# A hybrid GLA and mLSTM block: value blocks in tags of their own, values in four pieces, weight loads behind value transfers

## The chip, the cores and the metric

The kernel runs on one core of one Trainium2 chip. The metric is the device time of the core in microseconds (us). Engines: PE multiplies matrices, DVE, ACT and POOL work on vectors, SP issues most DMA transfers. Each engine works through its own instructions in the order of the program, and waits for another only through semaphores.

## The reference

One layer of a decoder trunk on 1024 tokens and 16 learned meta tokens in front (1040 rows of width 1024). Token mixing has two branches of four heads each, GLA and mLSTM, both in chunks of tokens that carry a matrix state on; then gates, a merge, and a feed-forward part with a causal convolution.

```python
# GLA, one chunk
inter = jnp.einsum('bhtk,bhkv->bhtv', qc * jnp.exp(bc), S)
scores = jnp.einsum('bhtk,bhsk,bhtsk->bhts', qc, kc, decay)
out = inter + jnp.einsum('bhts,bhsv->bhtv', scores, vc)
S_new = exp(b_last) * S + jnp.einsum('bhsk,bhsv->bhkv', kc * jnp.exp(b_last - bc), vc)
# mLSTM, one chunk
num = w_inter * jnp.einsum('bhtk,bhkv->bhtv', qc, C_prev) + jnp.einsum('bhts,bhsv->bhtv', qk, vc)
C_new = g_prev * C_prev + jnp.einsum('bhs,bhsk,bhsv->bhkv', w_state, kc, vc)
```

Both take values `v` of 256 columns per head, with tokens on the rows.

## The kernel before

Projections are computed with three matmuls per block of 128: the high part of the input by the high part of the weight (xH, wH), then xL by wH and xH by wL, in one accumulation. A weight block arrives as `wr` (512 KB, one DMA on SP, two buffers), ACT casts it to `wH` (L152), DVE subtracts to get `wL` (L153). That is `prep` (L141 to L153).

The stage of the heads takes the first 590 us. Its eight heads (0 to 3 GLA, 4 to 7 mLSTM) follow one another: `value_proj(s)` (it runs `proj_v`, L263), then `key_query_proj(s + 1)`. These are generators that PE works on at full density. At every `yield` the function `main` (L1226) adds a number to an account, `due`, and for every whole unit takes one step of other work (`advance`, L1214): one step of `closing` (`post`: scaling, turning and storing a finished head) and one of `side` (`gla` or `mlstm` of a head whose keys, queries and values are there). PACE is 1.15. A half piece of values counts `share` = 9/4 n/T, where n is the columns of the piece and T is 1040; its six pieces and halves yield twice each, which makes 10.35 steps for the values of a head, and the six yields of keys and queries make 6.9.

Values come out of `proj_v` with channels on the rows and have to be turned. Per head there are three pieces of the token axis, VSEG, of 400, 384 and 256 columns, and two halves of 128 channels (`j`). A half piece is 24 matmuls into `pv` (L281), an eviction by ACT into `vs` (L285), a turn of 32 x 32 blocks by DVE into `vr` (L287 and L288), stores of `vr` to DRAM on SP (L298, L301), and a load back into `v` (L306) with tokens on the rows. The `vr` blocks have the tag "r" with two buffers; the turned outputs `of` of `post` (L782) have the same tag, so a new `vr` waits for the stores of an `of` (L792), and the other way round.

In a GLA head the scores of a chunk are made by levels 1, 2, 4, ..., 64. A level is: two subtractions on DVE (L952, L953), an exponent on ACT (L954), a product in two halves on POOL and DVE (L956) and one on DVE (L957) that give `pk`; then four matmuls into `sc` on PE (L904), and a masked copy into A on DVE (L923). `sct` (L893) turns A when all levels up to 16 are in. After the last chunk `post` takes rstd of the head by POOL's power (L124), scales eight blocks on ACT (L773) and the row `om` (L774).

In an mLSTM head keys and queries go through a convolution of three operations on DVE (L1105), the rows MB and WB of the gates are broadcast from DRAM by SP (L1097, L1099), and then eight chunks follow: a state update matmul `up` (L1156), two output matmuls `op` (L1188, L1189), DVE's update of the state C (L1186) and copy of `dn` (L1191), ACT's copy and square (L1190, L1192). Two chunks are one step.

A scheduler sets the order of each engine from the order of the program, priorities (`hp`) and its own estimate of when things are ready; `behind_all` and `issue_after` keep an instruction behind another. The order is fixed when the program is built.

Of the kernel before, what the change touches and what calls it, by code (L numbers as in the profile page):

```python
# [9 lines left out]
F32 = mybir.dt.float32  # L10
# [7 lines left out]
P = 128  # L18
D = 1024
NM = 16  # L20
SEQ = 1024
T = NM + SEQ
NK = D // P
# [4 lines left out]
DV = 256  # L28
# [12 lines left out]
SEG_ALL = [(0, 272), (272, 256), (528, 256), (784, 256)]  # L41
# [4 lines left out]
def hybrid_kernel(ctx, tc, x, meta, norm_mix, w_in, b_in, gla_w_gate, gla_b_gate, gla_norm,  # L46
                  ml_conv_w, ml_conv_b, ml_norm, w_branch_gla, w_branch_ml, w_out, norm_ffn,
                  ffn_w_up, ffn_conv_w, ffn_conv_b, ffn_w_down, norm_final, out):
    nc = tc.nc
    x, out = x[0], out[0]  # L50
    w_in, b_in = w_in[0], b_in[0]
# [7 lines left out]
    def hp(n):  # L59

        return tc.high_priority(offset=max(1, min(n, tc.cur_priority - floor[0])))
# [56 lines left out]

    def rstd_of(ss, n, w, pool, name):

        v = pool.tile([P, w], F32, name=name + "v", tag="rv", bufs=4)
        nc.vector.tensor_scalar(v, ss, 1.0 / n, EPS, OP.mult, OP.add)
        r = pool.tile([P, w], F32, name=name + "r", tag="rr", bufs=4)
        rooted[:] = [nc.gpsimd.tensor_tensor(r, v, mhalf.to_broadcast([P, w]), OP.pow)]  # L124
        return r

# [6 lines left out]
    def behind_all(ins):  # L133
        es = ExitStack()
        for i in ins:
            es.enter_context(tc.issue_after(i))
        return es

    parted = []

    def prep(src, shape, name):  # L141

        if name == "gk1":
            raw = hd.tile([P, T], F32, name="wr_" + name, tag="raw", bufs=1)[:, :NK * P].rearrange(
                "p (k n) -> p k n", n=P)
        else:
            raw = wp.tile(shape, F32, name="wr_" + name, tag="wr", bufs=2)
        nc.sync.dma_start(raw, src)
        wH = wp.tile(shape, F32R, name="wH_" + name, tag="wH")
        wL = wp.tile(shape, F32R, name="wL_" + name, tag="wL")  # L150
        with behind_all(held):
            nc.scalar.activation(wH, raw, AF.Copy)  # L152
            parted[:] = [nc.vector.tensor_tensor(wL, raw, wH.bitcast(F32), OP.subtract).ins]  # L153
        return wH, wL
# [53 lines left out]
    def wsrc(w, k0, nk, n0, n):  # L208
        return w[k0 * P:(k0 + nk) * P, n0:n0 + n].rearrange("(k p) n -> p k n", p=P)
# [45 lines left out]
                    continue  # L255
                yield

    VSEG = [(0, 400), (400, 384), (784, 256)]
    hsc = dram.tile([NC, P, D], F32, name="hsc")
    vsc = [hsc[2 * (s % H):2 * (s % H) + 2].rearrange("a p (x w) -> (a p x) w", w=DV).rearrange("(b i) w -> b i w", i=32)  # L260
           for s in range(2 * H)]
# [1 line left out]
    def proj_v(s, us, vt):  # L263

        U.get(us[0])
        U.get(us[1], 1)
        due_load = []
        for g, (t0, n) in enumerate(VSEG):
            nb, b0 = n // 32, max(t0 - NM, 0) // 32
            at, share = 1 if g == 0 else 0, 9 / 4 * n / T  # L270
            R = hd.tile([P, T], F32, name=f"vr{s}_{g}", tag="r", bufs=2)[:, :64 * (nb + at)].rearrange(
                "p (b t j) -> p b t j", t=2, j=32)
            for j in range(2):
                wH, wL = U.got[us[j]]
                pt = ps.tile([P, 512], F32, name=f"pv{us[j]}_{g}", tag="pj", bufs=3)
                i = 0
                for k in range(NK):
                    if k == NK // 2:
                        yield share
                    for a, b in ((wH, xH), (wH, xL), (wL, xH)):  # L280
                        nc.tensor.matmul(pt[:, :n], a[:, k, :], b[:, k, t0:t0 + n], start=(i == 0), stop=(i == 3 * NK - 1))  # L281
                        i += 1
                with hp(PRI_E):
                    S = hd.tile([P, 400], F32, name=f"vs{us[j]}_{g}", tag="vs", bufs=2)
                    kept_ = nc.scalar.activation(S[:, :n], pt[:, :n], AF.Identity, bias=vbias[:, 2 * s + j:2 * s + j + 1])  # L285
                    if at:
                        nc.vector.transpose(R[:, 0, j, :], S[:, :32])  # L287
                    turned_ = nc.vector.transpose(R[:, at:, j, :], S[:, NM * at:n].rearrange("p (b j) -> p b j", j=32))  # L288
                    hold(turned_.ins, kept_.ins)
                    evicts.append(kept_.ins)  # L290
                if j == 0:
                    for load in due_load:
                        load()
                    due_load.clear()
                yield share
            for q in range(4):
                cols = slice(64 * q, 64 * q + 64)
                nc.sync.dma_start(vsc[s][b0:b0 + nb, :, cols].rearrange("b i w -> i b w"),  # L298
                                  R[32 * q:32 * q + 32, at:].rearrange("p b t j -> p b (t j)"))
                if at:  # L300
                    nc.sync.dma_start(vt[:NM, 0, cols], R[32 * q:32 * q + NM, 0].rearrange("p t j -> p (t j)"))  # L301

            def load(g=g, t0=t0, n=n):
                c = 0 if g == 0 else (t0 - NM) // P
                m = n // P
                nc.sync.dma_start(vt[:, 1 + c:1 + c + m, :DV],  # L306
                                  vsc[s][4 * c:4 * (c + m)].rearrange("(c b) i w -> (b i) c w", b=4))
            due_load.append(load)
        late_loads.extend(due_load)

# [39 lines left out]
    def rows(dst, ap, off, n):  # L350
        small.append((dst, bass.AP(tensor=ap.tensor, offset=ap.offset + off, ap=[[P, n], [1, P]])))

    va = hd.tile([P, DV + 1], F32, name="va", tag="S", bufs=4)[:, :P]
    segs = [(b_in, O_GQ, 8), (b_in, O_GR, 8), (b_in, O_MQ, 8), (b_in, O_MO, 8), (b_in, O_GA, 16), (gla_norm, 0, 2),
            (ml_conv_w, 0, 32), (ml_conv_b, 0, 8), (ml_norm, 0, 8)]
    at, nrow = [], 0
# [441 lines left out]
    A0 = hd.tile([P, P], F32, name="A0", tag="wg", bufs=1)  # L798

    def state(name):  # L800
        return hd.tile([P, DV + 1], F32, name=name, tag="S", bufs=4)

    def first_decay():

# [44 lines left out]
    def gla(s):  # L849
# [189 lines left out]
        up = upd(0)  # L1039
        om = hd.tile([2, DV + 1], F32, name=f"om{s}", tag="om", bufs=1)  # L1040
        ss = hd.tile([P, NC + 1], F32, name=f"ss{s}", tag="ss", bufs=2)
        junk = hd.tile([P, DV], F32, name=f"junk{s}", tag="junk", bufs=1)
        nc.vector.memset(ss, 1.0)
        yield
        op = ps.tile([P, 2, DV], F32, name=f"omp{s}", tag="ot", bufs=2)
# [39 lines left out]
    def mlstm(s):  # L1085
# [77 lines left out]
        om = hd.tile([2, W1], F32, name=f"om{s}", tag="om", bufs=1)  # L1163
        ss = hd.tile([P, NC + 1], F32, name=f"ss{s}", tag="ss", bufs=2)
        dn = hd.tile([P, NC + 1], F32, name=f"dn{s}", tag="dn", bufs=2)
        junk = hd.tile([P, DV], F32, name=f"junk{s}", tag="junk", bufs=1)
        nc.vector.memset(ss, 1.0)
        nc.vector.memset(dn, 1.0)
        up = upd(0)
# [54 lines left out]
    due = [0.0]  # L1224

    def main(gen, pace=PACE):  # L1226
        for share in gen:
            for load in late_loads:
                load()
            late_loads.clear()  # L1230
            due[0] += pace * (share or 1)
            while due[0] >= 1:
                due[0] -= 1
                advance()
# [3 lines left out]
    for s in range(8):  # L1238
        if s:
            side.append((gla if s < 4 else mlstm)(s))  # L1240
        if s == 3:
            side.append(small_rows())
        main(value_proj(s))
        if s < 7:
            main(key_query_proj(s + 1))
    for j in TAIL:
        main(merge_gate_b(j))
    while side or closing:
# [62 lines left out]
    def gate_weights(q):  # L1311

        rg, ru = (gs.tile([P, NK, P], F32, name=f"gw{i}{q}", tag="wr3") if (2 * q + i) % 3 == 2 else
                  wp.tile([P, NK, P], F32, name=f"gw{i}{q}", tag="wr", bufs=2) for i in range(2))
        for r, g in ((rg, GATES[2 * q]), (ru, GATES[2 * q + 1])):
            nc.sync.dma_start(r, wsrc(w_in, 0, NK, g[0], P))
        def split(src, h, l):
            nc.scalar.activation(h, src, AF.Copy)
            nc.vector.tensor_tensor(l, src, h.bitcast(F32), OP.subtract)

        def place(name):
            nonlocal ngw
            ngw += 1
            if ngw % 4 == 3:
                return [gs.tile([P, NK, P], F32R, name=f"g{p}{name}_{q}", tag="w4" + p) for p in "HL"]
            return [wp.tile([P, NK, P], F32R, name=f"g{p}{name}_{q}", tag="w" + p) for p in "HL"]

        def halves(t):
            return [(t[0][:, 4 * i:4 * i + 4], t[1][:, 4 * i:4 * i + 4]) for i in range(2)]
        a = WP[q] = {}  # L1330
        t = place("A1")
        split(rg, *t)
        a["A11"], a["A12"] = halves(t)
        yield
        s3 = gs.tile([P, 4, P], F32, name=f"gS3{q}", tag="S3")
        nc.vector.tensor_tensor(s3, rg[:, 0:4], ru[:, 0:4], OP.subtract)
        nc.vector.tensor_tensor(ru[:, 0:4], ru[:, 0:4], ru[:, 4:8], OP.add)
        a["S1"], a["S3"] = halves(place("SA"))
        split(ru[:, 0:4], *a["S1"])
        split(s3, *a["S3"])  # L1340
        yield
        nc.vector.tensor_tensor(rg[:, 0:4], ru[:, 0:4], rg[:, 0:4], OP.subtract)
        nc.vector.tensor_tensor(rg[:, 4:8], rg[:, 4:8], rg[:, 0:4], OP.subtract)
        t = place("SB")
        split(rg, *t)
        a["S2"], a["S4"] = halves(t)
        yield
        t = gs.tile([P, NK, P], F32R, name=f"gA22{q}", tag="A22")
        a["A22"] = t[:, 0:4], t[:, 4:8]
        split(ru[:, 4:8], *a["A22"])  # L1350
        yield
# [848 lines left out]
```

## Time and profile before

| | us |
|---|---|
| median of 3 runs (1851.85 to 1854.78) | 1853.07 |
| the profiled execution | 1852.45 |
| its span, first to last instruction | 1850.7 |
| PE busy in it | 1813.6 |
| mean granted clock of PE | 0.995 |

The profile is of one execution. A group of instructions is given by line, engine, operation and the tiles it writes and reads; "idle before" is the time its engine stood still just before it, with what ended that. PE is the engine that is nearly always busy, so a wait of PE is time of the kernel, and a wait of another engine is time only where PE waits for it in turn.

### The profile page before, as it was taken

What the parts mean: (1) busy time and instruction counts of PE and PEld (TensorE: products, weight loads), DVE (VectorE), ACT (ScalarE), POOL (GpSimd) and SP (SyncE); (2) the same over time, 40 slices, a digit from 0 to 9 for tenths busy, and PEclk for the clock granted to TensorE, in tenths of its full rate; (3) what the DMA queues carried; (4) which work ended last, traced back from release to release, by engine and by line L of the source; (5) the groups of instructions that cost most, each with busy time, mean ns of one, the idle gap of its engine ahead of it and who ended that gap; (6) DMA issues with size and microseconds to landing.
All of it is one profiled execution on the core that took longest, in us unless ns stands there. A gap on an engine that the chain in (4) does not pass through costs nothing. (4 is left out here: it accounts for less than half of the span.)

```text
span 1850.7 us, 31744 instructions
## 1 busy us (share of the span) xinstructions
PE 1813.6 (98%) x12630; PEld 1744.8 (94%) x12630; DVE 1254.6 (68%) x1843; ACT 867.1 (47%) x1402; POOL 444.0 (24%) x510
## 2 busy tenths in 40 slices
PE   8999999989999999999999999999999999999998
PEld 7899999989998999999999999999999999988886
DVE  7956767457762676664623647798887887787876
ACT  6565564635553443332512335544434433465664
POOL 5201111005540011134471710012222222200100
PEclk9999999999999999999999999999999999999999
DMA  5224234245443745556963743333333334398794
GB/s 158 67 72 95 55 85 99 64 112 157 141 124 101 206 149 152 168 179 183 356 207 120 258 155 115 114 109 120 114 104 109 114 110 125 93 341 310 282 379 165
DMA packets 288442, 285.45 MB, mean 154 GB/s; under 512 B 50882, under 2 KB 245773, under 8 KB 288295
## 3 DMA queue, kind: packets, MB, share of 16 engines
q1 hardware_dynamic: 266559, 212.08, 37.8%
q0 software_dynamic: 19136, 62.62, 9.7%
q10 hardware_dynamic: 2600, 8.74, 1.2%
q8 instruction: 99, 1.62, 0.4%
q14 instruction: 48, 0.39, 0.1%
HBM read 205.26 MB, written 77.99 MB: 153 GB/s over the span
## 5 line engine op out<-in xcount | busy, mean ns | idle before, releaser
L686 POOL TENSOR_TENSOR ts<-ts 128x256 f32<-128x256 f32 x88 | 78.6, 902 | 50.3 <-DMA ts<-in_ffn_w_down_dram 48.3
L1717 POOL TENSOR_TENSOR SB<-SA,rg 128x512 f32<-128x512 f32 x20 | 32.7, 1635 | 239.5 <-issue 101.5
L1804 PE MATMUL po<-wH_wo,yH 128*128 128x256 f32 x256 | 72.3, 283 | 0.1
L1804 PE MATMUL po<-wL_wo,yH 128*128 128x256 f32 x256 | 71.9, 282 | 0.3 <-DVE wL_wo L153 0.3
L1804 PE MATMUL po<-wH_wo,yL 128*128 128x256 f32 x256 | 72.0, 282 | 0.0
L281 PE MATMUL pv<-xH,wH_mv 128*128 128x400 f32 (+2 forms) x192 | 65.2, 339 | 0.4 <-ACT vs L285 0.4
L281 PE MATMUL pv<-xH,wH_gv 128*128 128x400 f32 (+2 forms) x192 | 65.6, 342 | 0.0
L1752 DVE SCALAR_TENSOR_TENSOR cv<-u,fc,cv 128x1024 f32<-128x1024 f32 x44 | 65.2, 1482 | 0.4
L1699 POOL TENSOR_TENSOR A<-u2raw,A 128x512 fp32r<-128x512 f32 x20 | 42.4, 2121 | 85.8 <-ACT A L1698 85.8
L281 PE MATMUL pv<-xL,wH_gv 128*128 128x400 f32 (+2 forms) x192 | 62.0, 323 | 0.0
L281 PE MATMUL pv<-xH,wL_gv 128*128 128x400 f32 (+2 forms) x192 | 61.9, 322 | 0.0
L281 PE MATMUL pv<-xL,wH_mv 128*128 128x400 f32 (+2 forms) x192 | 61.7, 321 | 0.0
L281 PE MATMUL pv<-xH,wL_mv 128*128 128x400 f32 (+2 forms) x192 | 61.5, 320 | 0.0
L1511 PE MATMUL bm<-omH,wH_bm 128*128 128x342 f32 x192 | 61.4, 320 | 0.0
L1511 PE MATMUL bm<-omH,wL_bm 128*128 128x342 f32 x192 | 61.3, 319 | 0.0
L1511 PE MATMUL bg<-ogH,wH_bg 128*128 128x342 f32 x192 | 61.3, 319 | 0.0
L1511 PE MATMUL bg<-ogH,wL_bg 128*128 128x342 f32 x192 | 61.2, 319 | 0.0
L1511 PE MATMUL bm<-omL,wH_bm 128*128 128x342 f32 x192 | 61.2, 319 | 0.0
L1511 PE MATMUL bg<-ogL,wH_bg 128*128 128x342 f32 x192 | 61.2, 319 | 0.0
L1698 ACT ACTIVATE HA<-rg 128x1024 fp32r<-128x1024 f32 x16 | 17.0, 1061 | 72.6 <-PE Yu L1258 72.3
L1287 ACT ACTIVATE u2raw<-Xu 128x258 f32<-128x258 f32 (+1 forms) x44 | 16.4, 374 | 69.0 <-PE Xu L1258 69.0
L1804 PEld LDWEIGHTS po<-wH_wo,yH 128*128 128x128 f32 x256 | 48.1, 188 | 0.6 <-DVE h L1811 0.3
(816 smaller groups left out, 7387.9 us busy)
## 6 DMA issues: line engine op xcount, KB each, us to landing
gw<-in_w_in_dram SPq DMA_DIRECT2D x26, 512.0 KB
ts<-in_ffn_w_down_dram POOLq DMA_DIRECT2D x44, 256.0 KB, 4.1
tdn<-ts POOLq DMA_DIRECT2D x44, 256.0 KB, 3.1
rg<-in_ffn_w_up_dram SPq DMA_DIRECT2D x22, 512.0 KB
ru<-in_ffn_w_up_dram SPq DMA_DIRECT2D x22, 512.0 KB
adr<-s SPq DMA_DIRECT2D x40, 256.0 KB
rd<-in_ffn_w_down_dram SPq DMA_DIRECT2D x20, 512.0 KB
do<-tdn SPq DMA_DIRECT2D x18, 512.0 KB
```

Of the source, the lines that this page charges most:

```text
L281: nc.tensor.matmul(pt[:, :n], a[:, k, :], b[:, k, t0:t0 + n], start=(i == 0), stop=(i == 3 * NK - 1))
L686: nc.gpsimd.tensor_tensor(t[:, o], t[:, a], t[:, b], OP.subtract)
L1287: evicted["U"] = nc.scalar.activation(u2, X[:, :n], AF.Copy).ins
L1511: nc.tensor.matmul(pt[:, i, :n], a[:, k, :], b[k][:, base + t0:base + t0 + n], start=(k == 0 and j == 0), stop=(k == NK - 1 and j == 2))
L1698: nc.scalar.activation(h, src, AF.Copy)
L1699: eng.tensor_tensor(l, src, h.bitcast(F32), OP.subtract)
L1717: late.tensor_tensor(sb[:, 0:4], sa[:, 0:4], rg[:, 0:4], OP.subtract)
L1752: nc.vector.scalar_tensor_tensor(y, u[:, j:SEQ + j], fc[:, j, jj:jj + 1], y, OP.mult, OP.add)
L1804: nc.tensor.matmul(pt[:, :DV], a, b[:, k % 4, :], start=(k == 0 and i == 0), stop=(k == NK - 1 and i == len(terms) - 1))
```

## The change

Values are cut in the four pieces of SEG_ALL (272, 256, 256 and 256 columns, 384 matmuls more in all). The turned blocks get tags of their own, `vr` (two buffers) and `vm` for the 16 meta rows; `vs` has one buffer of 272 columns. Stores and loads of the values get the high priority, and the last of them is kept in `moved`; weight loads of `prep` and of the gates are issued behind it. A half piece is one step of 24 matmuls, one `yield`, so the values of a head make 8 x 1.15 = 9.2 steps, and keys and queries 6 x 1.15 x 1.17 = 8.07. `rv` and `rr` have 2 buffers and the states 3, where they had 4; `junk` moves to the constants. Lines of the kernel behind L148 move by one to three.

```diff
     def prep(src, shape, name):
...
-        nc.sync.dma_start(raw, src)
+        with behind_all(moved):
+            nc.sync.dma_start(raw, src)
...
-    VSEG = [(0, 400), (400, 384), (784, 256)]
...
-        for g, (t0, n) in enumerate(VSEG):
+        for g, (t0, n) in enumerate(SEG_ALL):
             nb, b0 = n // 32, max(t0 - NM, 0) // 32
-            at, share = 1 if g == 0 else 0, 9 / 4 * n / T
-            R = hd.tile([P, T], F32, name=f"vr{s}_{g}", tag="r", bufs=2)[:, :64 * (nb + at)].rearrange(
-                "p (b t j) -> p b t j", t=2, j=32)
+            at = 1 if g == 0 else 0
+            R = hd.tile([P, 8, 2, 32], F32, name=f"vr{s}_{g}", tag="vr", bufs=2)
+            if at:
+                R0 = hd.tile([P, 2, 32], F32, name=f"vm{s}", tag="vm", bufs=1)
...
                 for k in range(NK):
-                    if k == NK // 2:
-                        yield share
...
-                    S = hd.tile([P, 400], F32, name=f"vs{us[j]}_{g}", tag="vs", bufs=2)
+                    S = hd.tile([P, 272], F32, name=f"vs{us[j]}_{g}", tag="vs", bufs=1)
...
-                        nc.vector.transpose(R[:, 0, j, :], S[:, :32])
-                    turned_ = nc.vector.transpose(R[:, at:, j, :], S[:, NM * at:n].rearrange("p (b j) -> p b j", j=32))
+                        nc.vector.transpose(R0[:, j, :], S[:, :32])
+                    turned_ = nc.vector.transpose(R[:, :, j, :], S[:, NM * at:n].rearrange("p (b j) -> p b j", j=32))
...
-                yield share
+                yield
             for q in range(4):
                 cols = slice(64 * q, 64 * q + 64)
...
+                with hp(PRI_E):
+                    moved[:] = [nc.sync.dma_start(vsc[s][b0:b0 + nb, :, cols].rearrange("b i w -> i b w"),
+                                                  R[32 * q:32 * q + 32].rearrange("p b t j -> p b (t j)")).ins]
...
     def main(gen, pace=PACE):
-        for share in gen:
+        for _ in gen:
...
-            due[0] += pace * (share or 1)
+            due[0] += pace
...
-            main(key_query_proj(s + 1))
+            main(key_query_proj(s + 1), PACE * 1.17)
...
-            nc.sync.dma_start(r, wsrc(w_in, 0, NK, g[0], P))
+            with behind_all(moved):
+                nc.sync.dma_start(r, wsrc(w_in, 0, NK, g[0], P))
```

The scheduler answers with another order. Three places are shown, before and after; a number behind a name is the head or the weight block, the last one counts tiles.

First pair: DVE at the end of head 4's values, where `wL_mq1`, a weight of head 5's queries, is made. Before:

```order
L288 STREAM_TRANSPOSE vr4_1_3414<-vs20_1_3488 128x12x32
L782 STREAM_TRANSPOSE of3_0_3472<-or3_0_3269 128x4x4x2x32
L782 STREAM_TRANSPOSE of3_1_3517<-or3_1_3270 128x4x4x2x32
L751 COPY tcol_436<-rtp0_3671 128x64
L751 COPY tcol_436<-rtp1_3677 128x64
L755 COPY tcol_436<-rtp2_3683 16x16
L756 COPY tcol_436<-rtp2_3683 2x4
L1105 SCALAR_TENSOR_TENSOR kc4_3730<-kT4_3002,col_113,kc4_3730 128x1040 x3
L288 STREAM_TRANSPOSE vr4_2_3503<-vs19_2_3537 128x8x32
L288 STREAM_TRANSPOSE vr4_2_3503<-vs20_2_3570 128x8x32
L153 TENSOR_TENSOR wL_mq1_3583<-wr_mq1_3580,wH_mq1_3582 128x1024
L153 TENSOR_TENSOR wL_mv1_0_3589<-wr_mv1_0_3586,wH_mv1_0_3588 128x1024
```

And now:

```order
L287 STREAM_TRANSPOSE vr4_3_3810<-vs19_3_3836 128x8x32
L738 TENSOR_TENSOR sr2_3717<-sr1_3716,sr2_3717 4x16
L741 TENSOR_TENSOR sr1_3716<-sr1_3716,sr2_3717 4x15
L287 STREAM_TRANSPOSE vr4_3_3810<-vs20_3_3873 128x8x32
L784 STREAM_TRANSPOSE of3_1_3876<-or3_1_3522 128x4x4x2x32
L753 COPY tcol_436<-rtp0_4019 128x64
L753 COPY tcol_436<-rtp1_4025 128x64
L757 COPY tcol_436<-rtp2_4031 16x16
L758 COPY tcol_436<-rtp2_4031 2x4
L154 TENSOR_TENSOR wL_mq1_3894<-wr_mq1_3891,wH_mq1_3893 128x1024
L154 TENSOR_TENSOR wL_mv1_0_3900<-wr_mv1_0_3897,wH_mv1_0_3899 128x1024
L154 TENSOR_TENSOR wL_mv1_1_3990<-wr_mv1_1_3987,wH_mv1_1_3989 128x1024
```

The turns of the last piece of `vr4` stood behind the convolutions `kc4` and now stand ahead of the copies of `rtp`; the convolutions stand behind the three weight subtractions.

Second pair: SP around the broadcasts MB4 and WB4 of head 4 and the load of `mq2`, a weight of head 6's queries. Before, amid the transfers of head 4's values (`vr4`, `v4`):

```order
L298 DMA hsc_100<-vr4_1_3414 32x12x64 x4
L792 DMA oscg_423<-of3_1_3517 32x8x128 x2
L306 DMA v4_3286<-hsc_100 128x3x256
L148 DMA wr_mv1_1_3689<-in_w_in_dram 128x8x128
L148 DMA wr_mk2_3797<-in_w_in_dram 128x8x128
L792 DMA oscg_423<-of3_1_3517 32x8x128 x2
L148 DMA wr_mq2_4148<-in_w_in_dram 128x8x128
L298 DMA hsc_100<-vr4_2_3503 32x8x64 x4
L1097 DMA MB4_3726<-rsc_429 128x1024
L148 DMA wr_mv2_0_4154<-in_w_in_dram 128x8x128
L306 DMA v4_3286<-hsc_100 128x2x256
L1099 DMA WB4_3728<-rsc_429 128x1024
```

And now, at the end of those of head 5:

```order
L298 DMA hsc_100<-vr5_2_4286 32x8x64 x2
L308 DMA v5_4109<-hsc_100 128x2x256
L298 DMA hsc_100<-vr5_2_4286 32x8x64 x2
L298 DMA hsc_100<-vr5_3_4387 32x8x64 x2
L308 DMA v5_4109<-hsc_100 128x2x256
L298 DMA hsc_100<-vr5_3_4387 32x8x64 x2
L149 DMA wr_mq2_4492<-in_w_in_dram 128x8x128
L149 DMA wr_mv2_0_4498<-in_w_in_dram 128x8x128
L308 DMA v5_4109<-hsc_100 128x2x256
L1099 DMA MB4_4067<-rsc_429 128x1024
L1101 DMA WB4_4069<-rsc_429 128x1024
L149 DMA wr_mv2_1_4653<-in_w_in_dram 128x8x128
```

The load of `mq2` stood ahead of the last stores of `vr4` and now stands behind those of `vr5`; MB4 and WB4 have moved past all transfers of `v5`.

Third pair: ACT at the end of head 1 (`or1`, `rs1r` are its outputs and scales) and the start of head 2's levels (`pk2_2`, `pk2_4`). Before:

```order
L285 ACTIVATE vs11_0_2085<-pv11_0_2046,vbias_115 128x400
L954 ACTIVATE pk2_2_2149<-pk2_2_2149 128x1024
L1074 ACTIVATE or1_1_1978<-op1_3_2089 128x512
L1077 ACTIVATE junk1_1971,ss1_1970<-or1_1_1978 128x256 x2
L954 ACTIVATE pk2_4_2179<-pk2_4_2179 128x1024
L773 ACTIVATE or1_0_1977<-or1_0_1977,rs1r_2114 128x256 x4
L285 ACTIVATE vs12_0_2135<-pv12_0_2099,vbias_115 128x400
L773 ACTIVATE or1_1_1978<-or1_1_1978,rs1r_2114 128x256 x4
L774 ACTIVATE om1_1969<-om1_1969,rs1r_2114 2x256
L954 ACTIVATE pk2_8_2207<-pk2_8_2207 128x1024
L285 ACTIVATE vs11_1_2203<-pv11_1_2166,vbias_115 128x384
```

And now:

```order
L1076 ACTIVATE or1_1_2130<-op1_3_2245 128x512
L1079 ACTIVATE junk1_2097,ss1_2096<-or1_1_2130 128x256 x2
L284 ACTIVATE vs11_1_2289<-pv11_1_2264,vbias_115 128x256
L775 ACTIVATE or1_0_2129<-or1_0_2129,rs1r_2295 128x256 x4
L775 ACTIVATE or1_1_2130<-or1_1_2130,rs1r_2295 128x256 x3
L284 ACTIVATE vs12_1_2329<-pv12_1_2304,vbias_115 128x256
L775 ACTIVATE or1_1_2130<-or1_1_2130,rs1r_2295 128x256
L776 ACTIVATE om1_2095<-om1_2095,rs1r_2295 2x256
L956 ACTIVATE pk2_2_2342<-pk2_2_2342 128x1024
L956 ACTIVATE pk2_4_2384<-pk2_4_2384 128x1024
L284 ACTIVATE vs11_2_2380<-pv11_2_2355,vbias_115 128x256
L956 ACTIVATE pk2_8_2424<-pk2_8_2424 128x1024
```

The exponents of levels 2 and 4 stood ahead of the scalings by `rs1r` and now stand behind all eight and the row `om1`.

More of the change, by code (lines that the diff above doesn't have):

```diff
@@ L119, in rstd_of @@
     def rstd_of(ss, n, w, pool, name):
-        v = pool.tile([P, w], F32, name=name + "v", tag="rv", bufs=4)
+        v = pool.tile([P, w], F32, name=name + "v", tag="rv", bufs=2)
         nc.vector.tensor_scalar(v, ss, 1.0 / n, EPS, OP.mult, OP.add)
-        r = pool.tile([P, w], F32, name=name + "r", tag="rr", bufs=4)
+        r = pool.tile([P, w], F32, name=name + "r", tag="rr", bufs=2)
         rooted[:] = [nc.gpsimd.tensor_tensor(r, v, mhalf.to_broadcast([P, w]), OP.pow)]
@@ L137, in behind_all @@
         return es
-    parted = []
+    parted, moved = [], []
     def prep(src, shape, name):
@@ L294, in proj_v @@
                     due_load.clear()
-                yield share
+                yield
             for q in range(4):
                 cols = slice(64 * q, 64 * q + 64)
[L298 to L301, printed above, removed]
+                with hp(PRI_E):
+                    moved[:] = [nc.sync.dma_start(vsc[s][b0:b0 + nb, :, cols].rearrange("b i w -> i b w"),
+                                                  R[32 * q:32 * q + 32].rearrange("p b t j -> p b (t j)")).ins]
+                    if at:
+                        moved[:] = [nc.sync.dma_start(vt[:NM, 0, cols],
+                                                      R0[32 * q:32 * q + NM].rearrange("p t j -> p (t j)")).ins]
             def load(g=g, t0=t0, n=n):
@@ L305, in load @@
                 m = n // P
-                nc.sync.dma_start(vt[:, 1 + c:1 + c + m, :DV],
-                                  vsc[s][4 * c:4 * (c + m)].rearrange("(c b) i w -> (b i) c w", b=4))
+                with hp(PRI_E):
+                    moved[:] = [nc.sync.dma_start(vt[:, 1 + c:1 + c + m, :DV], vsc[s][4 * c:4 * (c + m)].rearrange(
+                        "(c b) i w -> (b i) c w", b=4)).ins]
             due_load.append(load)
@@ L351, in rows @@
         small.append((dst, bass.AP(tensor=ap.tensor, offset=ap.offset + off, ap=[[P, n], [1, P]])))
-    va = hd.tile([P, DV + 1], F32, name="va", tag="S", bufs=4)[:, :P]
+    va = hd.tile([P, DV + 1], F32, name="va", tag="S", bufs=3)[:, :P]
     segs = [(b_in, O_GQ, 8), (b_in, O_GR, 8), (b_in, O_MQ, 8), (b_in, O_MO, 8), (b_in, O_GA, 16), (gla_norm, 0, 2),
@@ L800, in state @@
     def state(name):
-        return hd.tile([P, DV + 1], F32, name=name, tag="S", bufs=4)
+        return hd.tile([P, DV + 1], F32, name=name, tag="S", bufs=3)
     def first_decay():
@@ L1041, in gla @@
         ss = hd.tile([P, NC + 1], F32, name=f"ss{s}", tag="ss", bufs=2)
-        junk = hd.tile([P, DV], F32, name=f"junk{s}", tag="junk", bufs=1)
+        junk = const.tile([P, DV], F32, name=f"junk{s}", tag="hj", bufs=1)
         nc.vector.memset(ss, 1.0)
@@ L1165, in mlstm @@
         dn = hd.tile([P, NC + 1], F32, name=f"dn{s}", tag="dn", bufs=2)
-        junk = hd.tile([P, DV], F32, name=f"junk{s}", tag="junk", bufs=1)
+        junk = const.tile([P, DV], F32, name=f"junk{s}", tag="hj", bufs=1)
         nc.vector.memset(ss, 1.0)
```

## The prediction

> **What bounds the kernel now.** I read the page's head first, then busy time in stretches, then the waits of the stretch that the change touches.
>
> ```profile
> span 1850.7 us, 31744 instructions
> PE 1813.6 (98%) x12630; PEld 1744.8 (94%) x12630; DVE 1254.6 (68%) x1843; ACT 867.1 (47%) x1402; POOL 444.0 (24%) x510
> ```
>
> PE is busy 98% of the span, so time can go only into or out of PE's holes (37 us in all), or into PE's own work. Where the holes lie, by stretches (busy us and count of each engine, granted clock, DMA share):
>
> ```profile
> core 0: us, PE busy (x) PEld busy (x) DVE busy (x) ACT busy (x) POOL busy (x), PEclk, DMA share, GB/s
> 66.00:160.00 94.00, 87.01 (x531) 82.19 (x531) 69.79 (x114) 50.46 (x93) 15.53 (x14) 0.98 0.23 58
> 160.00:320.00 160.00, 157.27 (x984) 151.33 (x983) 109.07 (x168) 92.52 (x184) 21.37 (x26) 1.00 0.37 90
> 320.00:480.00 160.00, 153.27 (x906) 147.89 (x905) 89.95 (x144) 82.72 (x163) 37.82 (x41) 0.98 0.41 108
> 480.00:600.00 120.00, 114.81 (x697) 109.53 (x696) 63.20 (x100) 54.79 (x115) 42.48 (x41) 0.99 0.46 126
> 600.00:1851.00 1251.00, 1240.42 (x9091) 1198.20 (x9089) 872.64 (x1224) 544.45 (x774) 292.01 (x326) 1.00 0.54 179
> ```
>
> The four stretches of 66 to 600 us, where the heads run, hold 7.0 + 2.7 + 6.7 + 5.2 = 21.6 us of PE idle. After 600 us PE's order does not change. So about 21 us is the most that the change could win, and the waits of that stretch name it (us in total, times, longest):
>
> ```profile
> engine line waited for: us in total, times, longest us
> PE sc L904 <- DVE pk L957: 7.1, 5, 3.0
> PE pj L241 <- DVE wL_mq L153: 5.5, 1, 5.5
> PE up L1156 <- DMA v<-hsc: 2.8, 1, 2.8
> PE sct L893 <- DVE A L923: 1.8, 1, 1.8
> PE k0t L1128 <- ACT qc L1112: 1.5, 2, 0.8
> PE pj L241 <- ACT vs L285: 0.8, 1, 0.8
> PE pv L281 <- ACT vs L285: 0.4, 1, 0.4
> ```
>
> **What goes.** The 5.5 us stand at one place, at the end of head 4's values:
>
> ```profile
> 369.59 3.97 DVE L1105 SCALAR_TENSOR_TENSOR kc<-kT,col,kc 128x1040 f32<-128x1040 f32 x3 [0.29 <-ACT kc L1103]
> 373.48 0.77 DVE L288 STREAM_TRANSPOSE vr<-vs 128x256 f32<-128x256 f32 x2
> 374.17 1.18 DVE L153 TENSOR_TENSOR wL_mq<-wr_mq,wH_mq 128x1024 fp32r<-128x1024 f32 x1
> ```
>
> DVE works in order. The two turns of the last piece wrote into a block under the tag that the turned outputs `of` use too, so they were placed late, behind three convolutions, and the subtraction that PE waited for stood behind them. With a tag of its own the block is free early: in the new DVE order (first pair of excerpts above) the turns come first, then `wL_mq1`, then the convolutions. What is late next is ACT: `wH_mq1` now stands behind the last of three evictions of the keys.
>
> ```profile
> 359.10 1.05 ACT L152 ACTIVATE wH_mv<-wr_mv 128x1024 fp32r<-128x1024 f32 x1
> 367.87 0.55 ACT L624 ACTIVATE kT<-pj,col 128x346 f32<-128x346 f32 x1 [3.27 <-PE pj L241]
> 584.95 0.60 SPq L306 DMA_DIRECT2D v<-hsc  x1
> ```
>
> Eviction 0.55 + cast 1.05 = 1.6 us, then 1.18 on DVE; PE meanwhile has the transposes `rtp` and six matmuls that need only wH. I leave 1.0 of the 5.5, a gain of **4.5**. The 2.8 us are the last load of v7, issued at 584.95 behind a weight load; it now stands ahead of the weights: **2.8** gained. The evictions L285 that waited (1.2) lay behind one run of scalings; their pieces are shorter now and their place in ACT's order is their own: **1.2** gained. Sum of gains: 8.5 us.
>
> **What the pieces cost.** 384 more matmuls, the same columns. First and last of 48 matmuls of 384 columns and of 48 of 256:
>
> ```profile
> 340.43 0.34 PE L281 MATMUL pv<-xH,wH_mv 128*128 128x384 f32 x1
> 348.72 0.34 PE L281 MATMUL pv<-xH,wL_mv 128*128 128x384 f32 x1
> 478.78 0.28 PE L281 MATMUL pv<-xH,wH_mv 128*128 128x256 f32 x1
> 484.30 0.28 PE L281 MATMUL pv<-xH,wL_mv 128*128 128x256 f32 x1
> ```
>
> 8.29/47 = 176.4 ns and 5.52/47 = 117.4 ns: 59 ns for 128 columns, and nothing left over at zero columns (117.4 - 2 x 59 = -0.6). So a split costs between 0 and some 3 ns a matmul, 0 to 1.2 us; I take **+0.5**. The Trainium skill, "TensorE: Matmul & The Clock Gate", section "Back-to-back issue gap", says otherwise: sustained spacing of 81 ns at 128 columns and 131 ns at 512, a fixed share for the weight load of about 64 ns by my estimate from these two, by which 384 more matmuls would cost some 25 us. The two pitches above contradict it for this kernel.
>
> **Weights behind values.** A weight of head 5 or 6 that used to be loaded early is now issued behind the last stores of the values (second pair of excerpts). For `mq2` the load comes in time, but its cast stands behind the last key eviction, and here no `rtp` lies between: 0.55 + 1.05 us, and 1.18 on DVE against six matmuls of 0.16: **+1.9**; for `mq3` the same with more before it, **+0.5**. Ends: 0 (the scheduler's order hides it) and +4 (the load is late).
>
> **The levels of the scores.** This term is the one to get right: 7.1 + 1.8 us today. A level on DVE is the following run (head 2), and on PE a piece between two levels:
>
> ```profile
> 213.40 0.58 DVE L288 STREAM_TRANSPOSE vr<-vs 128x384 f32<-128x384 f32 x1 [0.41 <-ACT vs L285]
> 213.90 0.38 DVE L956 TENSOR_TENSOR pk<-pk,kT 128x256 f32<-128x256 f32 x1
> 214.20 0.68 DVE L957 TENSOR_TENSOR pk<-pk,qT 128x512 f32<-128x512 f32 x1
> 214.80 0.75 DVE L952 TENSOR_TENSOR pk<-bc 128x256 f32<-128x256 f32 x2
> 215.47 0.68 DVE L953 TENSOR_TENSOR pk<-bc 128x512 f32<-128x512 f32 x1
> 216.08 0.71 DVE L923 COPY_PREDICATED A<-mu,sc 128x512 f32<-128x512 uint8 x1
> ```
>
> From 213.40 to the end of the last is 3.4 us. PE now has 24 x 117.4 ns = 2.8 us and its own scores (0.9) between levels: 3.7 us, so an undisturbed DVE just keeps up. It is disturbed where the closing of the head before runs into it:
>
> ```profile
> 204.49 1.06 ACT L954 ACTIVATE pk<-pk 128x1024 f32<-128x1024 f32 x1 [1.28 <-DVE pk L953]
> 206.47 1.71 ACT L773 ACTIVATE or<-or,rs1r 128x256 f32<-128x256 f32 x4 [0.92 <-POOL rs1r L124]
> L773 ACT ACTIVATE or<-or,rs1r 128x256 f32<-128x256 f32 x8 | 3.4, 497 | 0.9 <-POOL rs1r L124 0.9
> L957 DVE TENSOR_TENSOR pk<-pk,qT 128x512 f32<-128x512 f32 x24 | 26.0, 1085 | 0.6 <-ACT pk L954 0.6
> L956 POOL TENSOR_TENSOR pk<-pk,kT 128x256 f32<-128x256 f32 (+1 forms) x24 | 26.9, 1124 | 78.6 <-ACT pk L954 78.5
> ```
>
> Before, the exponents of head 2's first two levels (the second at 204.49) ran ahead of the scalings of head 1 (206.47); now they stand behind all eight (third pair of excerpts). From the last chunk of head 1 to the first scaling it took about 5.2 us; then eight scalings 3.4, an eviction and the row `om` 1.0, the exponent 1.06, POOL's half of the product 1.1 to 1.4, L957 0.7 to 1.2: the pair is ready 12.5 to 13.5 us after that chunk. PE comes to it after three pieces, a column sum and a fourth piece, 4 x 2.8 + 0.5 = 11.8 us: a wait of about 2 us, today 0.4 at most: **+1.7**. In head 1 PE comes after three pieces, the sum and 0.6 us, at 9.6: a wait of 3.5 us; the longest of today, 3.0, is in this head: **+0.5**. Heads 0 and 3 have denser steps today and even ones then, but with a fourth turn per head on DVE: I take **+0.9** between -3 and +3.
>
> **Steps that clump.** The broadcasts MB4 and WB4 of head 4 moved in SP's queue behind the transfers of head 5 (second pair of excerpts), and head 4's chunks now follow one another in PE with three convolutions between DVE's state updates.
>
> ```profile
> 466.01 0.59 PE L1156 MATMUL up<-v,KT 128*128 128x257 f32 x2
> 468.18 0.60 PE L1189 MATMUL op<-C,WB 128*128 128x257 f32 x2
> L1186 DVE SCALAR_TENSOR_TENSOR C<-C,gp,up 128x257 f32<-128x257 f32 x28 | 13.4, 479 | 33.6 <-PE up L1156 33.4
> ```
>
> Two chunks start their six matmuls between 466.01 and 468.18, 0.43 us each, 1.3 a chunk; DVE needs 0.48 + 0.15 a chunk and 1.3 for a convolution, so 1.9 in three of seven. Wait about 1.3 us here, and 1.0 at head 6 where the first chunk needs the late row WB6: **+2.3**, between 0 and +6.
>
> **Sum:** -8.5 + 0.5 + 2.4 + (1.7 + 0.5 + 0.9) + 2.3 = -0.2 us against this execution's 1852.45 us (0.6 below the median shown, 1853.07). The forecast is no change, **1852.3 us**; differences below 0.2% (3.7 us) are about what a measurement of this kernel cannot tell from none.
>
> **Rivals.** *The closing takes over the levels (slower).* ACT's scalings ahead of the exponents hold POOL, DVE and PE in turn. If L957 takes its 1.2 us and not 0.7 (its mean is 1.085), POOL 1.4, and the copies of A come behind them, each of the levels behind the late one is late too: the even pace of 3.7 us leaves no slack to catch up. Two levels in each of four heads at 0.9 us more give +7: 1859.5. It decides once a level costs DVE over 3.7 us. For it: 7.1 us of waits on this line today; against it: L957 took 0.68 at 214.20, alone. *The even pace pays (faster).* 24 matmuls between levels instead of 12 cover what today waits 7.1 + 1.8: if heads 0 and 3 lose most of their waits (-3), and the clumps are covered (-2.3), the sum is -5.5: 1847. For it: the 21 us and the spacing; against it: heads 1 and 2 by the order. *Fixed price per matmul (slower).* If each matmul had a part that does not shrink with the columns, 40 ns of the 117.4 would do for +15: 1868; the two pitches speak against it. The spacing of the Trainium skill above is this case. *The tags don't part.* If the turns still waited for stores, the 4.5 would stay: 1857, inside the range; the order speaks against it.
>
> **Numbers.** Forecast 0.38; even pace 0.31; closing 0.26, the tags 0.03, fixed price 0.02. Hence faster 0.31, within 0.2% 0.38, slower 0.31. The range takes in both rivals and the ends of the clumps and of the weights: 1844.5 to 1861.
>
> **What would show it.** Right: no wait of PE for `wL_mq` over 1.5 us and none for v near 585; new waits for wH of `mq2`, and for `pk` in head 2 of about 2 us; values at 117 ns a matmul. Wrong: a wait of 5 us in head 1 or 2, or over 3 us amid head 4's chunks; or PE idle between 66 and 600 us below 17 or above 27.

## The result, and the profile after

The changed kernel takes 1859.29 us (median of 11 runs, 1856.18 to 1865.07), the kernel before, beside it, 1851.86 us (11 runs, 1849.9 to 1854.78): ratio 1.0038, 95% interval 1.0028 to 1.0048. It is slower by 7 us. The time lies in the range of the forecast, but the forecast said no change.

The profiled execution of the changed kernel took 1865.07 us, the longest of its eleven. It shows the causes enlarged: its span is 12.6 us longer than the one before, where the medians are 7.4 apart. Of its page the head, and of its busy time the stretches of the heads:

```profile
span 1863.3 us, 32591 instructions
PE 1822.6 (98%) x13014; PEld 1753.7 (94%) x13014; DVE 1244.3 (67%) x1859; ACT 870.6 (47%) x1418; POOL 436.6 (23%) x510
```

```profile
66.00:160.00 94.00, 86.73 (x605) 82.65 (x604) 66.18 (x113) 48.31 (x93) 14.80 (x13) 0.93 0.22 56
160.00:320.00 160.00, 154.56 (x1034) 147.94 (x1034) 107.24 (x174) 92.45 (x182) 22.25 (x25) 0.98 0.32 83
320.00:480.00 160.00, 151.42 (x1003) 144.80 (x1002) 78.08 (x130) 79.16 (x152) 21.39 (x29) 0.97 0.34 91
```

The columns are those of before. Read the last but two, the granted clock of PE: 0.93, 0.98 and 0.97, where it was 0.98, 1.00 and 0.98. The waits of PE from 66 to 620 us:

```profile
PE sc L906 <- DVE pk L959: 9.7, 3, 4.5
PE pj L242 <- ACT wH_mq L153: 4.7, 2, 3.1
PE k0t L1130 <- ACT qc L1114: 2.3, 2, 1.3
PE sct L895 <- DVE A L925: 1.9, 1, 1.9
PE u L1162 <- issue: 1.4, 1, 1.4
PE pv L280 <- ACT vs L284: 1.1, 1, 1.1
PE pj L242 <- ACT vs L284: 1.0, 1, 1.0
PE sc L875 <- ACT kq L868: 0.8, 2, 0.7
PE up L1158 <- DVE C L1188: 0.6, 1, 0.6
```

The wait for wL of mq (5.5) and the one for v (2.8) are gone, as forecast. In their place stand wH of mq (4.7) and longer waits for pk (9.7, was 7.1), now at three places. All rows of this view, with three small ones left out here, come to 24.3 us; before, all came to 21.4. That is 3 us more, far from 12.6.

The rest is in how PE runs behind a wait. Here is the longest, in head 1 (PE: start, duration and operation):

```profile
143.18 0.28 PE L280 MATMUL pv<-xL,wH_gv 128*128 128x256 f32 x1
148.00 0.55 PE L906 MATMUL sc<-pk 128*128 128x128 f32 x1 [4.54 <-DVE pk L959]
...
150.06 0.41 PE L280 MATMUL pv<-xH,wH_gv 128*128 128x256 f32 x1
150.27 0.41 PE L280 MATMUL pv<-xL,wH_gv 128*128 128x256 f32 x1
...
153.11 0.28 PE L280 MATMUL pv<-xH,wH_gv 128*128 128x256 f32 x1
153.23 0.28 PE L280 MATMUL pv<-xL,wH_gv 128*128 128x256 f32 x1
```

Behind the wait the same matmuls start 0.21 us apart, and only from about 152.9 on 0.12 us apart again: 4.9 us at some half of the pace, which costs about 2 us more. The granted clock of PE is 0.50 from 146.08 to 152.91, so this is the clock.

Between the first and the last matmul the granted clock is 0.50 in eight stretches after, in which PE is busy for 31.4 us, and in three before, with 11.4 us (one of the eight, at 13 us, lies ahead of the heads). A matmul at 0.21 us and not 0.12 loses 0.43 of its time, which by estimate makes 13.5 us lost after and 4.9 before, 8.6 more. The heads of the two pages agree: of the 12.6 us, PE's busy time takes 9.0 (1813.6 to 1822.6) and its idle time 3.6. Of the 9.0 the pieces explain 1.5 (384 times 127 + 3 x 118 - 183 - 176 - 118 = 4 ns, the median distances of the two traces), so 7.5 are left for matmuls at a slower pace, in line with the estimate. Of the 3.6, 2.9 are the waits above, and 0.7 stay unassigned.

Which wait is followed by such a stretch can be read as well. In each profile the stretches begin on a grid of 3.41 us and last one step of it or two. Here is that grid around a wait for pk in head 2 that is 2.1 us long in two kernels, the change (first two rows) and e1 of the experiments below (last three); the columns are those of before:

```profile
217.76:221.17 3.41, 1.48 (x13) 1.27 (x11) 3.41 (x6) 2.57 (x4) 2.26 (x3) 1.00 0.32 73
221.17:224.59 3.42, 3.24 (x15) 3.27 (x16) 3.42 (x8) 0.00 (x0) 0.00 (x0) 0.50 0.06 14
216.19:219.60 3.41, 2.20 (x19) 2.00 (x17) 3.41 (x6) 2.87 (x5) 2.15 (x3) 1.00 0.36 83
219.60:223.02 3.42, 2.54 (x22) 2.57 (x23) 3.42 (x7) 0.40 (x1) 0.18 (x1) 1.00 0.00 0
223.02:226.43 3.41, 3.41 (x32) 3.41 (x31) 3.41 (x7) 1.45 (x3) 0.30 (x1) 1.00 0.52 118
```

In the change, PE stands still for 1.9 us of one step, and the next step runs at 0.50. In e1 a border of the grid parts the wait into 1.2 and 0.9 us, and the clock stays at 1.00. It is so in all twelve profiles of this case, from 60 to 1260 us: each of the 30 steps at full clock in which PE stood still for 1.74 us or more was followed by a step at 0.50, none of some 3000 with less than 1.5 us was, and of the 20 between these 6 were. Where the grid lies against the kernel differs between profiles, so the same wait can cost its length in one execution and 1.5 to 3 us more in another (0.43 of one step or two).

Why head 1 waits is on ACT:

```profile
139.93 2.91 ACT L775 ACTIVATE or<-or,rs0r 128x256 f32<-128x256 f32 x7 [2.38 <-POOL rs0r L124]
142.74 0.45 ACT L284 ACTIVATE vs<-pv,vbias 128x256 f32<-128x256 f32 x1
143.10 0.50 ACT L775 ACTIVATE or<-or,rs0r 128x256 f32<-128x256 f32 x1
143.50 0.49 ACT L776 ACTIVATE om<-om,rs0r 2x256 f32<-2x256 f32 x1
143.90 1.99 ACT L956 ACTIVATE pk<-pk 128x1024 f32<-128x1024 f32 x2
```

ACT stands still for 2.38 us, waiting for POOL's power, then scales for 4 us, and only at 143.90, without a gap behind them, come the exponents that PE has been waiting for since 143.5. With the scalings behind them (e2, below, where this part comes 2.6 us earlier) two of them have ended by 138.3.

### The profile page after: what moved, and what is told of

Read it like the earlier page. It is cut to its first block, busy times and chain, and to the rows that moved or that the text cites. A ratio compares the mean times of both kernels' runs of the same rounds, so it can differ in the third digit from the quotient of the medians.

```text
span 1863.3 us, 32591 instructions
## 1 busy us (share of the span) xinstructions
PE 1822.6 (98%) x13014; PEld 1753.7 (94%) x13014; DVE 1244.3 (67%) x1859; ACT 870.6 (47%) x1418; POOL 436.6 (23%) x510
## 5 line engine op out<-in xcount | busy, mean ns | idle before, releaser
L280 PE MATMUL pv<-xH,wH_gv 128*128 128x256 f32 (+1 forms) x256 | 77.0, 301 | 0.0
L280 PE MATMUL pv<-xH,wH_mv 128*128 128x256 f32 (+1 forms) x256 | 75.9, 296 | 1.1 <-ACT vs L284 1.1
L280 PE MATMUL pv<-xH,wL_gv 128*128 128x256 f32 (+1 forms) x256 | 74.3, 290 | 0.0
L280 PE MATMUL pv<-xL,wH_gv 128*128 128x256 f32 (+1 forms) x256 | 73.8, 288 | 0.0
L280 PE MATMUL pv<-xL,wH_mv 128*128 128x256 f32 (+1 forms) x256 | 73.5, 287 | 0.0
L280 PE MATMUL pv<-xH,wL_mv 128*128 128x256 f32 (+1 forms) x256 | 73.1, 285 | 0.0
L284 ACT ACTIVATE vs<-pv,vbias 128x256 f32<-128x256 f32 (+1 forms) x64 | 30.2, 472 | 67.7 <-PE pv L280 58.9
L280 PEld LDWEIGHTS pv<-xH,wH_gv 128*128 128x128 f32 x256 | 50.4, 197 | 0.5
```

## The experiments

**Theory A:** the loss is new waits of PE at single places, by the order on ACT (scalings ahead of exponents; casts of late weights), and each long wait is followed by a slow stretch of about 2 us. **Rivals:** the dense steps of 24 matmuls or the pieces themselves cost it (B); weights and values, unordered, would collide on SP (C). Each run is a ratio to the kernel before, run beside it on the same chip.

| run | built from | median us | ratio (95% interval) |
|---|---|---|---|
| the change | | 1859.29 | 1.0038 (1.0028 to 1.0048) |
| e1_weights_free | the change | 1860.81 | 1.0048 (1.0035 to 1.0060) |
| e2_late_scalings | the change | 1845.90 | 0.9968 (0.9956 to 0.9981) |
| e6_free_late | e1 and e2 | 1851.81 | 1.0001 (0.9992 to 1.0010) |
| e3_half_steps | the change | 1853.19 | 1.0012 (1.0003 to 1.0020) |
| b1_before_late | before | 1846.50 | 0.9974 (0.9965 to 0.9984) |
| e9_one_tag_late | e2 | 1847.46 | 0.9981 (0.9972 to 0.9990) |
| e10_pace_late | e2 | 1864.44 | 1.0074 (1.0061 to 1.0086) |
| e11_half_late | e2 and e3 | 1844.45 | 0.9962 (0.9949 to 0.9974) |
| e12_mq_free | e11 | 1846.53 | 0.9968 (0.9955 to 0.9981) |
| e13_half_late_free | e11 | 1854.10 | 1.0007 (0.9998 to 1.0016) |

### Weight loads free again (e1)

```diff
-        with behind_all(moved):
-            nc.sync.dma_start(raw, src)
+        nc.sync.dma_start(raw, src)
```

(and the same for the gate weights)

> The changed kernel, but weight loads are not issued behind the value transfers. Theory A (the loss is new waits of PE, and after each long wait PE runs at about half pace for some 5 us, which costs about 2 us more): the waits of PE for wH of mq1 and mq2 (3.1 and 1.6 us after the change) and the slow stretches behind them go, 5 to 9 us of the changed kernel's 1859.3: 1850 to 1854. Rival B (the loss is in the dense steps of 24 matmuls and the four pieces themselves): within 2 us of 1859. Rival C (weights and values collide on SP when not ordered): the wait for v near 585 us comes back, 2.8 us, and the time is 1856 or more.

1.0048: nothing gained. The waits for wH of mq are gone. Those for pk are as they were, and the one for the convolved queries, at most 1.3 us in the change, has grown (waits of PE):

```profile
PE sc L905 <- DVE pk L958: 9.6, 3, 4.6
PE k0t L1129 <- ACT qc L1113: 6.0, 2, 5.1
```

The 5.1 us stand near 502 us: the weights now come early, ACT's casts and DVE's subtractions of two blocks run ahead of the convolution of an mLSTM head's queries, and PE waits for that. For the casts of late weights theory A fails here: loading the weights behind the values costs nothing net. Rival B's number fits, and says no more than that. Rival C's time fits too (1856 or more), but not its cause: no wait for v near 585 has come back.

### The closing two steps later (e2)

```diff
     def post(s, oraw, om, sc):
...
+        if s < 3:
+            yield
+            yield
         for c in range(NC):
             o = oraw[c // 4][:, DV * (c % 4):DV * (c % 4 + 1)]
             nc.scalar.activation(o, o, AF.Copy, scale=sc[:, c + 1:c + 2])
```

> The changed kernel, but the closing of heads 0 to 2 starts two steps later, so that on ACT the exponents of levels 2 and 4 of the next head stand ahead of the eight scalings, as before the change. Theory A: PE's waits for pk in heads 1 to 3 (4.5, 2.1 and 3.0 us) fall to 1 us or less each, and the slow stretches of about 2 us behind them go: 8 to 13 us less than the changed kernel, 1847 to 1852. Rival B (DVE cannot keep up with a level in 3.7 us, whatever stands ahead): the waits only move to a later level, and the time stays within 3 us of 1859.

1845.9 us: 13 us below the change and 0.32% below the kernel before. ACT in head 1 now:

```profile
135.60 1.06 ACT L959 ACTIVATE pk<-pk 128x1024 f32<-128x1024 f32 x1 [0.68 <-DVE pk L958]
137.21 1.06 ACT L959 ACTIVATE pk<-pk 128x1024 f32<-128x1024 f32 x1 [0.54 <-DVE pk L958]
138.17 0.46 ACT L284 ACTIVATE vs<-pv,vbias 128x256 f32<-128x256 f32 x1
138.53 3.30 ACT L778 ACTIVATE or<-or,rs0r 128x256 f32<-128x256 f32 x8
```

The exponents fill the time in which ACT had waited for POOL, and the scalings follow without a wait. PE's waits and the busy time by stretches:

```profile
PE pj L242 <- ACT wH_mq L153: 4.2, 2, 2.6
PE sct L898 <- DVE A L928: 2.7, 2, 1.8
PE k0t L1133 <- ACT qc L1117: 2.2, 2, 1.3
...
PE sc L909 <- DVE pk L962: 0.8, 1, 0.8
```

```profile
66.00:160.00 94.00, 89.97 (x655) 85.76 (x655) 70.53 (x121) 50.92 (x96) 19.08 (x14) 1.00 0.23 60
160.00:320.00 160.00, 158.87 (x1081) 151.93 (x1080) 107.56 (x172) 96.10 (x194) 21.46 (x26) 1.00 0.34 89
```

9.7 us of waits for pk became 0.8, 8.9 us; the gain is 13, so some 4 us more came with it. The clock reads 1.00 and 1.00 where it read 0.93 and 0.98, and of eight stretches at 0.50 one is left, of 3.4 us. The waits have not moved to a later level either, as the rival in the text above has it. The pieces and steps are unchanged, so rival B is out as the main cause; whether the dense steps brought the order about is not shown by this run.

### Both (e6)

> Both edits together: weight loads not behind the value transfers, and the closing of heads 0 to 2 two steps later. Theory A: the two gains add up, 1840 to 1846, below both kernels. Rivals: no better than the better one of the two alone.

1851.8 us: the edits do not add up, the free weights cost 6 us here. The wait of 5.1 us for the convolved queries is there again, and its slow stretch. Behind the value transfers is the better place for the weights: this part of the change is a gain that e1 alone could not show.

### Half steps (e3)

```diff
                 for k in range(NK):
+                    if k == NK // 2:
+                        yield 0.5
...
-                yield
+                yield 0.5
...
-            due[0] += pace
+            due[0] += pace * (share or 1)
```

> The changed kernel, but a half piece of 24 matmuls is two steps of half the weight, so the same 9.2 steps of attention are handed out every 12 matmuls. Theory A: ACT's order of scalings and exponents changes in heads 1 and 3 in part, the casts of mq1 and mq2 not at all; between 1854 and 1861. Rival B (the density of the steps is the cause): back to the time before, 1850 to 1854, with PE's waits for pk at 3 us or less in all.

1853.2 us, by the ratios 5 us better than the change and near the kernel before: below theory A's range, inside rival B's in time. Waits for pk fell to 5.9 us, and not below 3; those for wH of mq rose to 7.7. Steps of 12 matmuls let the first exponent of heads 1 and 3 ahead of the scalings (133.6 against 136.1 us, and 273.0 against 279.1), so the run does not tell density from order.

### The late closing on the kernel before (b1)

> The kernel before (three pieces, turned blocks under the shared tag), with only the closing of heads 0 to 2 two steps later. It tells whether the gain of the late closing belongs to the change. Theory A: before the change the exponents of head 2 stood ahead of the scalings already and those of heads 1 and 3 nearly so; the waits for pk (7.1 us in all, longest 3.0) can shrink by 3 to 5 us, with a slow stretch of 2 us: 1846 to 1851. Rival (the late closing is worth as much here as in the changed kernel, 13 us): 1840 or less.

1846.5 us, the same edit of `post` in the kernel before: 4.6 us gained, inside theory A's range and far from the rival's 13. Its waits:

```profile
PE pj L241 <- DVE wL_mq L153: 5.5, 1, 5.5
PE up L1159 <- DMA v<-hsc: 2.8, 1, 2.8
PE sc L907 <- DVE pk L960: 1.9, 2, 1.5
```

With the closing late in both, the kernel before has 0.9974 and the change 0.9968. So apart from the order of scalings and exponents, the change moves the time by some 1 us, with about 3 us to each side not excluded. The two long waits that the change removes are still there in this run, so the change pays elsewhere for having removed them.

### One tag, another pace, half steps, each with the late closing (e9, e10, e11)

```diff
# e9
-            R = hd.tile([P, 8, 2, 32], F32, name=f"vr{s}_{g}", tag="vr", bufs=2)
+            R = hd.tile([P, T], F32, name=f"vr{s}_{g}", tag="r", bufs=2)[:, :512].rearrange(
+                "p (b t j) -> p b t j", t=2, j=32)
# e10
-            main(key_query_proj(s + 1), PACE * 1.17)
+            main(key_query_proj(s + 1), PACE)
```

> The changed kernel with the late closing, but the turned value blocks under the tag of the turned outputs again. Theory A (own tags are worth the wait for wL of mq, 5.5 us before the change): a wait of 3 us or more comes back at the end of head 4's values or later, and the time is 3 to 8 us above the 1845.9 of the late closing: 1849 to 1854. Rival (the tags are worth nothing once the turns come ahead in the order): within 2 us of 1846.

1847.5 us, 1.6 above e2, with intervals that overlap. Waits for wL of mq come to 2.1 us and there is one of 2.4 us before the scores of an mLSTM head. The tags are worth less than the 5.5 us that they were to remove: the rival is nearer.

> The changed kernel with the late closing, but keys and queries hand out steps at the pace of values (6.9 a head instead of 8.07). Theory A (time is in waits at single places): the same waits for pk, and 1844 to 1850. Rival (denser steps in keys and queries are needed so that a head is done in time): steps are left over at the end of the heads and PE waits there, over 1850.

1864.4 us, the largest effect of all, 18.5 us, and theory A did not see it. The rival has the time (over 1850), but its place, the end of the heads, fits little more than the wait for wL of gb (3.3 us, at 572). PE's waits:

```profile
PE pj L242 <- ACT wH_mq L153: 8.2, 3, 5.6
PE k0t L1133 <- ACT qc L1117: 4.7, 2, 3.9
PE pj L242 <- DVE wL_gb L154: 3.3, 1, 3.3
PE k0t L1132 <- ACT kc L1116: 2.9, 1, 2.9
PE pj L242 <- DVE wL_mq L154: 2.7, 1, 2.7
```

With 1.17 left out, 9.2 + 6.9 = 16.1 steps are handed out per head, with it 17.3, as many as before the change (10.35 + 6.9). So the number of steps per head matters; that it decides whether the work of a head meets the casts and convolutions of the next is my reading of these waits, and not shown.

> The changed kernel with the late closing and steps of 12 matmuls at half the weight. Theory A: waits for pk stay below 2 us in all; the wait for wH of mq3 that half steps alone had (5.6 us) stays: 1846 to 1852. Rival (finer steps help by themselves, as in the run without the late closing, 6 us): 1840 to 1844.

1844.5 us, the fastest of all, though its interval overlaps that of e2, and between the ranges of the two texts. No wait for pk is left; those for wH of mq are 7.9 us, the longest 5.8.

### The weights of the queries alone (e12), and all (e13)

```diff
-        with behind_all(moved):
+        with behind_all([] if name.startswith("mq") else moved):
             nc.sync.dma_start(raw, src)
```

> The changed kernel with the late closing and half steps (1844.5), and of the weight loads only those of the queries of heads 5 to 7 (mq1, mq2, mq3) not behind the value transfers, so that ACT casts them ahead of the evictions of the keys. Theory A: PE's waits for wH of mq (7.9 us in all, longest 5.8) go, with one or two slow stretches of 2 us: 1834 to 1839, unless another wait takes the place. Rival (as with all weight loads free, the time comes back as a wait for the convolved queries of some 5 us): 1843 to 1847.

1846.5 us, ratio 0.9968: no gain on e11. The 7.9 us are gone, and others stand there (waits of PE, then ACT around the longest):

```profile
PE pj L242 <- ACT vs L286: 4.1, 1, 4.1
PE up L1163 <- ACT C L1169: 2.1, 1, 2.1
PE u L1167 <- DVE KT L1144: 1.8, 1, 1.8
```

```profile
476.45 2.10 ACT L780 ACTIVATE or<-or,rs5r 128x256 f32<-128x256 f32 x5 [9.61 <-DVE rs5r L1210]
478.46 0.45 ACT L286 ACTIVATE vs<-pv,vbias 128x256 f32<-128x256 f32 x1
```

No cast stands there. ACT has five scalings of head 5 ahead of the eviction that PE needs, and they wait, through DVE, for POOL's power of that head, which starts at 473.3 us though its input is ready at 467.1: POOL has other work first. It is what held up head 1, in a head that the late closing (heads 0 to 2) leaves as it was. Theory A in its plain form, take a wait away and gain it, fails here; the rival's time holds, with another wait than it named.

> The same with no weight load behind the value transfers. Theory A: the waits for wH of mq go, but the wait of PE for the convolved queries (5.1 us in both earlier runs with free weight loads) comes: 1840 to 1847. Rival (that wait came from the dense steps, not from the weight loads): 1834 to 1839.

1854.1 us: 8 us worse than e12, with the wait for `vs` (4.0) and a new one for the state of an mLSTM head (3.7), ahead of which DVE stood still 2.6 us for the broadcast WB. Neither of the two texts had these places.

## Why the prediction was wrong

**The bound** was right in its place: PE, between 66 and 600 us, nothing after that. But it looked for time in PE's holes and in added work only, and most of the 12.6 us lie in busy time at a slower pace.

**What goes:** the waits for wL of mq and for v went, 8.3 us. Of the 1.0 us that were to be left at mq1 there are 3.1. The step took the weight to be there when ACT came to the cast; it was not:

```profile
379.42 0.55 ACT L626 ACTIVATE kT<-pj,col 128x346 f32<-128x346 f32 x1 [3.27 <-PE pj L242]
382.46 1.06 ACT L153 ACTIVATE wH_mq<-wr_mq 128x1024 fp32r<-128x1024 f32 x1 [2.49 <-DMA wr_mq<-in_w_in_dram]
```

ACT itself waits 2.49 us for the load, which was behind the last stores on SP. The 1.2 us for `vs` did not go either: 1.1 and 1.0. So of the 8.5 us forecast, 2.4 + 2.8 - 0.9 = 4.3 came.

**Pieces:** +0.5 forecast, 1.5 by the median distances; 256 columns still take 118 ns and 272 take 127, so the rival of a fixed price is out. The spacing that the Trainium skill gives ("TensorE: Matmul & The Clock Gate", section "Back-to-back issue gap") would have cost some 25 us, an estimate from its two figures; the trace does not agree.

**Weights behind values:** mq2 as forecast (1.9; it was 4.7 - 3.1 = 1.6), mq3 no wait.

**The levels:** the mechanism was right. Head 1: 3.5 forecast, 4.5 measured; head 2: 2, 2.1, by luck, as the times given there (12.5 to 13.5 against 11.8) make 0.7 to 1.7; head 3: under "heads 0 and 3" with 0.9 for both, 3.0 measured. Head 0 was spared: its waits for pk are gone. The two waits together went from 8.9 to 11.6 us, +2.7 for 3.1 forecast, because the misses cancel. The rival "the closing takes over the levels" had the place right. Its price, 1859.5, came true by luck: it adds up two late levels in each of four heads, where there is one long wait in each of heads 1 to 3 and the clock behind it. e2 shows it.

**Clumps:** 2.3 forecast; the waits for C and for wt come to less than 1, and a wait of 1.4 before `u` is new.

**The step that failed** is the sum: a wait was priced at its own length, and the pace behind it at nothing. What the runs showed in its place is 7.5 us of slower matmuls in the profiled execution. The second miss is the size of "What goes": 4.3 us and not 8.5, so the waits came to +2.9 in all where the sum has -8.5 + 2.4 + 3.1 + 2.3 = -0.7. By waits and pieces alone the profiled execution would be 4.4 us slower, near the edge of what a measurement tells from no change; it is 12.6. In the median run, 7.4 us slower, some 3 are left for the pace, if its waits are those of the profile. The clocks agree with that: the median run has 0.993 and the profiled one 0.990, which on 1860 us is 5.6 us, and their spans are 5.7 apart.

The signs that the prediction named came out as for a right forecast: no wait for wL of mq or for v, a wait of 2.1 us in head 2, values at 118 ns, PE idle for 24.5 us between 66 and 600. All of them watch waits, pieces and holes, and none the clock, although the clock of 0.98 in two stretches of the profile of before was quoted. The Trainium skill, "TensorE: Matmul & The Clock Gate", section "What's actually happening", describes it: PE's clock is halved after an idle window of about 3.4 us, and the window runs freely. The half clock, the step of 3.41 us and the shifting place of the grid agree with the traces. A whole idle window was not needed: 1.74 us within one were enough.

**What stays open:** the price of a wait by itself was not tried, by adding a wait of known length at a quiet place; it is read from start times, from the granted clock and from e2's gain exceeding its waits. Nor were the number of steps and the four pieces tried alone on the kernel before.

## What to carry to other kernels

On an engine that works in order, an instruction that waits (the scalings for POOL's power) takes everything behind it along: put it behind work that is ready and that the bound engine needs, even if it is itself in no hurry; an edit of three lines gained 13 us in one kernel and 4.6 in another. Price a hole in PE by its length and, where it is longer than some 1.5 us, by the slow stretch that may follow it, and look at the granted clock of the stretch first. And a wait taken away counts only when the next one at the same place is known: in four runs (e1, e6, e12, e13) a wait for a cast was replaced by one of 4 to 5 us for a convolution or an eviction.

## What was not expected of the hardware

Behind many waits of 1.6 to 5.8 us PE's granted clock is 0.50 for 3.41 or 6.83 us, and matmuls of 256 columns start 0.21 us apart instead of 0.12. Not the length of the wait alone decides it, but how much of it falls into one step of a grid of 3.41 us: 1.74 us or more were always followed by half clock, less than 1.5 us never. Of the waits of 2.8 us and more in the kernel before, the change and e1, eight of nine were followed by it; the ninth (head 3 in e1, 3.0 us) lies across a border of the grid, with about 1.5 us on each side. The same kernel, with its many waits near 2 to 3 us, therefore spreads over 9 us in eleven runs of the change, against 5 us before: the mean clocks of the eleven go from 0.990 to 0.995, and 0.005 of 1860 us is 9.
